# Two plain tile pairs behind the first six tiles of each FFN, with their weights, sums and output weights issued earlier

## The chip, the cores and the metric

The kernel runs on one core of one Trainium2 chip. The metric is device time in microseconds (us), the median of several runs; the kernel before takes 1227.42 us (three runs, 1227.06 to 1229.53). A profile is one further execution with its own time.

## The reference

One encoder layer runs over two independent sequences of 256 tokens, 1024 features, in float32:

```python
def encoder_layer(x, ...):
    x = x + 0.5 * swiglu(rmsnorm(x, g_ffn1), w_ffn1_in, w_ffn1_out)
    h = rmsnorm(x, g_mix)
    (q, k, v, r, lr, ml_qk, ml_v, ml_o, ml_if, gate_a, gate_b) = split(h @ w_in)
    o_a = gla_mixer(...)      # chunked linear attention, both directions, 4 heads
    o_b = mlstm_mixer(...)    # chunked mLSTM, both directions, 4 heads
    x = x + (sigmoid(gate_a) * o_a + sigmoid(gate_b) * o_b) @ w_out
    return x + 0.5 * swiglu(rmsnorm(x, g_ffn2), w_ffn2_in, w_ffn2_out)

def swiglu(h, w_in, w_out):   # w_in 1024 x 5632, w_out 2816 x 1024
    a, g = split(h @ w_in, 2)
    return (silu(a) * g) @ w_out
```

The result is `rmsnorm(x, g_final)` for each sequence. The change concerns the two FFNs (swiglu) and the passage from the mixers to the second.

## The kernel before

Activations are held transposed, features on 128 partitions and the 512 tokens of both sequences in the columns, as eight tiles `x[k]`. TensorE works on float32 in a rounded form (fp32r). To keep precision each operand is split into a high part (ScalarE's rounding copy, `split2` L223) and a low part (VectorE's difference, L224), and each product takes three matmuls: high by high, high by low, low by high (`mm3`, L201 to L204).

An FFN (`ffn`, L312) has 22 pairs of tiles: pair j is tile 2j of `a` and tile 2j + 1 of `g`, each 128 of the 2816 inner features.

*First tiles.* Pairs 0 to 2 are computed plainly (`first_tiles`, L226): six PSUM banks, eight k slices, and for each k 18 matmuls of 512 columns on `split_x(k)`, the input times its gain but not yet normalized. The weights come in four raw tiles of two slices (`kp`), and their split goes to a `wa` pair. Meanwhile the squares of x are summed (ScalarE squares, GpSimd adds, L199), and `rms_stat` (L176) turns them into `r`, the reciprocal root of each token's mean square: a matmul with ones (L160), a few small operations, four diagonals and another matmul (L173), and a copy. It is issued at high priority.

*Units.* Pairs 3 to 21 are each one step of a Winograd form of Strassen's product, called a unit here (L341 to L366). It takes seven products of 256 columns in place of eight: 7 x 4 x 3 = 84 matmuls (`product`, L296). It needs sums of the normalized inputs, `x_sums` (L248), four steps of VectorE and ScalarE work that need `r`, and sums of the pair's weights, `w_sums` (L276): three loads, VectorE sums (L286 to L289), splits, and, for the two blocks that are used unsummed, a low part made by ScalarE's negated copy (L284) and an accumulating DMA that adds the weights again from memory (L285, issued by GpSimd). The products go to banks `y`, `z` and `q`. Two products of a unit, `finish(late, 0)` and `finish(late, 1)`, run inside the next one.

*Output tiles.* After pairs 0 to 7, 8 to 14 and 15 to 21 the eight tiles of the output product are accumulated over that part's activations `hs` and added to x (L371 to L385).

What orders the work: the kernel is written in one sequence, and a planner places each engine's instructions by that sequence (earlier is more urgent), by its own estimate of times and by the buffers that are free. Each engine then runs its list in order and waits where an input is late. Buffers that the steps below touch: `slab`, 44 tiles of 512 columns (split inputs, sums, split activations); `tmp`, 7 tiles; PSUM with four banks `acc` and four `sc` (`acc(..., True)`); and in an FFN two each of `raw`, `sum` (loads, 3 x 512 columns), `wa` (high and low, 5 x 512) and `wb` (2 x 512).

Loads are issued on SP's queue, accumulating DMAs on GpSimd's. The mixers use other pools (`wp`, three each of raw, high, low weights) in the memory that the FFN pools leave. After the last mixer step comes the product with `w_out` (L816 to L820), and then the pools are changed back and the second FFN's first weights loaded (L824 to L833):

```python
    for i in range(KD):
        ps = gemm(w_out[i], ms, f"wo{i}", i % 2 == 1)
        nc.vector.tensor_tensor(out=x[i], in0=ps, in1=x[i], op=ALU.add)
        xs2.append(split_x(i, C_G2, sq_of("b"), "b"))
    mixer_stage.close()
    last_stage = ExitStack()
    last_stage.enter_context(pools(**ffn_pools))
    raw2 = []
```

Of the kernel before, what the change touches and what calls it, by code (L numbers as in the profile page):

```python
# [9 lines left out]
F32 = mybir.dt.float32  # L10
# [26 lines left out]
def encoder_kernel(ctx: ExitStack, tc: tile.TileContext, xT, par, w2, gnorm, mask,  # L37
# [117 lines left out]
    def rms_cols(parts, cs, name):  # L155

        ps = scp(f"st_{name}", (P, len(cs)))
# [8 lines left out]
    def spread(r, name):  # L166
# [5 lines left out]
        ps = scp(f"sp_{name}", (P, n * P))  # L172
# [53 lines left out]
    def first_tiles(raws, xs_of, name):  # L226
# [3 lines left out]
        for kp in range(4):  # L230
            raw = raws[kp].rearrange("p i m f -> p i (m f)")
            whi, wlo = (t.rearrange("p a b -> p (a b)")[:, :2 * NF * P].rearrange("p (i f) -> p i f", i=2)
                        for t in w_pair("wa", 5, f"{name}{kp}"))
            for i in range(2):
                k = 2 * kp + i
                split2(whi[:, i], wlo[:, i], raw[:, i])
# [3 lines left out]
                for m in range(NF):  # L240
                    nc.tensor.matmul(pss[m], lhsT=whi[:, i, f[m]], rhs=xh, start=k == 0, stop=False)
                for m in range(NF):
                    nc.tensor.matmul(pss[m], lhsT=wlo[:, i, f[m]], rhs=xh, start=False, stop=False)
                for m in range(NF):
                    nc.tensor.matmul(pss[m], lhsT=whi[:, i, f[m]], rhs=xl, start=False, stop=k == KD - 1)
        return pss

    def x_sums(gcol, r, name):  # L248

        res = [[] for _ in range(7)]  # L250
        b11 = None
        for k in range(4):
            u, v, t, w = (tmp(f"x{c}_{name}{k}") for c in "uvtw")
# [18 lines left out]
        return res  # L272
# [39 lines left out]
    def ffn(w_a, w_o, xs_of, raws, gcol, sq, name, done, last=None):  # L312

        pss = first_tiles(raws, xs_of, f"{name}i")
        r, _ = rms_stat(sq, name)
        sums = {n: w_sums(w_a, n, f"{name}s{n}") for n in (NF // 2,)}
        xc = x_sums(gcol, r, name)
        hs = []
        for j in range(NF // 2):
            t, g = tmp(f"{name}t{j}"), tmp(f"{name}g{j}")  # L320
            nc.vector.tensor_tensor(out=t, in0=pss[2 * j], in1=r, op=ALU.mult)  # L321
            nc.scalar.activation(t, t, AF.Silu)
            nc.vector.tensor_tensor(out=g, in0=pss[2 * j + 1], in1=r, op=ALU.mult)
            hs.append(activate(t, g, f"{name}{j}"))
        L, R = slice(0, SEQ), slice(SEQ, T)
        add = lambda o, p, q: nc.vector.tensor_tensor(out=o, in0=p, in1=q, op=ALU.add)
        late = None
# [10 lines left out]

        parts = [range(0, 8), range(8, 15), range(15, KF)]
        for part in parts:  # L340
            for j in part:  # L341
                if j < NF // 2:
                    continue
                w = sums.pop(j)
                if j + 1 < KF:
                    sums[j + 1] = w_sums(w_a, j + 1, f"{name}s{j + 1}")
                y, z = acc(f"psy_{name}{j}"), acc(f"psz_{name}{j}")
                m, u = tmp(f"{name}m{j}"), tmp(f"{name}u{j}")
                t, g = tmp(f"{name}t{j}"), tmp(f"{name}g{j}")
                product(y, w[0], xc[X11], True, False)  # L350
                nc.scalar.copy(m[:, L], y[:, :SEQ])  # L351
                product(z, w[1], xc[X21], True, True)
                add(t[:, L], z[:, :SEQ], m[:, L])
                nc.scalar.activation(t[:, L], t[:, L], AF.Silu)
                if late:
                    finish(late, 0)
                product(y, w[4], xc[XT2], False, False)
                nc.scalar.copy(u[:, R], y[:, :SEQ])
                if late:
                    finish(late, 1)  # L360
# [600 lines left out]
```

## Time and profile before

| | us |
|---|---|
| median of three runs | 1227.42 |
| the profiled execution | 1228.9 |
| its span, first to last instruction | 1227.1 |
| TensorE busy (matmuls) | 1183.4 |
| VectorE busy | 763.8 |
| ScalarE busy | 609.6 |
| GpSimd busy | 105.6 |

Busy time of TensorE counts each matmul from its start to its modelled end, and matmuls overlap, so a busy TensorE is not yet at its best rate; starts of neighbouring matmuls show the rate. In order of time the span holds: loads to 8 us, the first FFN to 377, the mixers to 805, the product with `w_out` to 850, the second FFN to 1206, and the final norm. In the rows, PE is TensorE's matmul, PEld its weight load, DVE VectorE, ACT ScalarE, POOL GpSimd, SP the queue that issues loads; L302 is line 302 of the kernel. Names carry f1 or f2 for the FFN, with `xh_a` or `xh_b` for the split inputs, `xch` and `xcl` for input sums, `wah`/`wal` and `wbh`/`wbl` for the high and low parts in `wa` and `wb`, and `ps_f1i`, `ps_f1o` for the banks of the first and of the output tiles.

### The profile page before, as it was taken

To read this page: it belongs to the slowest core of one execution; us is meant where nothing else is said; L and a number is where in the kernel's file an instruction comes from. 1 tells how busy PE (TensorE), PEld (TensorE's weight loads), DVE (VectorE), ACT (ScalarE), POOL (GpSimd) and SP (SyncE) were. 2 spreads that over 40 slices of the span, in tenths; PEclk is the share of its full clock that TensorE was granted. 3 is DMA by queue.
4 is the path that set the end of the run, shared out by engine and by line. 5 is a ranking of instruction groups with operands and counts; after the bars stand their busy time and mean duration, and the time that the engine had idled before them with its cause. 6 is when DMAs were issued, how large, how long until landed. Compare 5 with 4: busy or idle time off the path is not lost.

```text
span 1227.1 us, 17179 instructions
## 1 busy us (share of the span) xinstructions
PE 1183.4 (96%) x6795; PEld 1031.8 (84%) x6795; DVE 763.8 (62%) x1159; ACT 609.6 (50%) x997; POOL 105.6 (9%) x118
## 2 busy tenths in 40 slices
PE   7899999999999999999999999999989999999996
PEld 6788899889987887888888888887889899889985
DVE  6976367547645879657564463464987357656643
ACT  5655156426535655565762332343565156426541
POOL 4000000000012002111000000012000001000011
PEclk9889999999999999999999999998999999999998
DMA  7346356445523313232223333314355346535512
GB/s 235 78 115 161 103 123 166 124 120 130 149 84 107 89 50 99 80 114 61 95 77 103 95 95 112 95 60 132 86 128 155 101 116 161 141 101 145 154 45 69
DMA packets 56801, 136.65 MB, mean 111 GB/s; under 512 B 5192, under 2 KB 19528, under 8 KB 56720
## 3 DMA queue, kind: packets, MB, share of 16 engines
q1 hardware_dynamic: 48480, 110.38, 28.7%
q0 software_dynamic: 6432, 22.81, 10.9%
q10 hardware_dynamic: 1808, 2.36, 0.6%
q8 instruction: 53, 0.87, 0.3%
q14 instruction: 28, 0.23, 0.1%
HBM read 133.42 MB, written 2.11 MB: 110 GB/s over the span
## 4 chain that ended last, share of the span: by engine, by line
PE 86%; DVE 8%; ACT 2%; DMA 2%; issue 1%; POOL 0%; POOLq 0%; DVEq 0%; SPq 0%; ACTq 0%
PE psy_f L302 17%; PE psq_f L302 8%; PE psz_f L302 4%; PE ps_f1o L202 3%; PE ps_f1o L203 3%; PE ps_f1o L204 3%; PE ps_f2o L203 3%; PE ps_f2o L202 3%; PE ps_f2o L204 3%; PE pt_ga L465 2%; PE pt_ga L464 2%; PE pt_ga L466 2%; PE pt_gb L465 2%; PE pt_gb L464 2%; PE pt_gb L466 2%
## 5 line engine op out<-in xcount | busy, mean ns | idle before, releaser
L302 PE MATMUL psy_f<-xch_f,wah_f1s 128*128 128x256 f32 x228 | 65.2, 286 | 3.8 <-DVE f1t L321 1.4
L302 PE MATMUL psy_f<-xch_f,wal_f2s 128*128 128x256 f32 x228 | 64.9, 285 | 4.2 <-DMA wal_f2s<-in_w_f 4.2
L302 PE MATMUL psy_f<-xch_f,wah_f2s 128*128 128x256 f32 x228 | 64.5, 283 | 0.1
L302 PE MATMUL psy_f<-xcl_f,wah_f2s 128*128 128x256 f32 x228 | 64.5, 283 | 0.0
L302 PE MATMUL psy_f<-xch_f,wal_f1s 128*128 128x256 f32 x228 | 64.5, 284 | 0.0
L302 PE MATMUL psy_f<-xcl_f,wah_f1s 128*128 128x256 f32 x228 | 64.3, 282 | 0.0
L464 PE MATMUL pt_ga<-whi_ga,xh_m 128*128 128x512 f32 x128 | 50.7, 396 | 0.0
L465 PE MATMUL pt_ga<-wlo_ga,xh_m 128*128 128x512 f32 x128 | 50.7, 396 | 0.0
L465 PE MATMUL pt_gb<-wlo_gb,xh_m 128*128 128x512 f32 x128 | 50.6, 396 | 0.0
L464 PE MATMUL pt_gb<-whi_gb,xh_m 128*128 128x512 f32 x128 | 50.5, 394 | 0.0
L466 PE MATMUL pt_ga<-whi_ga,xl_m 128*128 128x512 f32 x128 | 50.4, 393 | 0.0
L466 PE MATMUL pt_gb<-whi_gb,xl_m 128*128 128x512 f32 x128 | 50.2, 393 | 0.0
L94 DVE TENSOR_TENSOR wlo_ga<-raw_ga,whi_ga 128x1024 fp32r<-128x1024 f32 x16 | 19.6, 1225 | 46.3 <-ACT whi_ga L93 46.3
L302 PEld LDWEIGHTS psy_f<-xch_f,wah_f1s 128*128 128x128 f32 x228 | 43.7, 192 | 5.0 <-DVE f1t L321 1.7
L302 PEld LDWEIGHTS psy_f<-xch_f,wal_f2s 128*128 128x128 f32 x228 | 43.4, 190 | 4.6 <-DMA wal_f2s<-in_w_f 4.6
L385 DVE SCALAR_TENSOR_TENSOR x<-ps_f2o,x 128x512 f32<-128x512 f32 x23 | 15.9, 690 | 49.2 <-PE ps_f2o L204 49.2
L385 DVE SCALAR_TENSOR_TENSOR x<-ps_f1o,x 128x512 f32<-128x512 f32 x24 | 16.6, 690 | 44.3 <-PE ps_f1o L204 44.3
L302 PEld LDWEIGHTS psy_f<-xcl_f,wah_f1s 128*128 128x128 f32 x228 | 43.8, 192 | 0.1
L302 PEld LDWEIGHTS psy_f<-xch_f,wah_f2s 128*128 128x128 f32 x228 | 43.3, 190 | 0.6 <-ACT f2m L351 0.5
L302 PEld LDWEIGHTS psy_f<-xch_f,wal_f1s 128*128 128x128 f32 x228 | 43.6, 191 | 0.0
L302 PEld LDWEIGHTS psy_f<-xcl_f,wah_f2s 128*128 128x128 f32 x228 | 43.3, 190 | 0.1
L94 DVE TENSOR_TENSOR wlo_gb<-raw_gb,whi_gb 128x1024 fp32r<-128x1024 f32 x16 | 19.6, 1223 | 36.1 <-ACT whi_gb L93 36.0
(1085 smaller groups left out, 4043.2 us busy)
## 6 DMA issues: line engine op xcount, KB each, us to landing
raw_f1s<-in_w_f SPq DMA_DIRECT2D x19, 512.0 KB, 3.7
wal_f1s<-in_w_f POOLq DMA_DIRECT2D x19, 512.0 KB, 5.6
raw_f2s<-in_w_f SPq DMA_DIRECT2D x19, 512.0 KB, 3.7
wal_f2s<-in_w_f POOLq DMA_DIRECT2D x19, 512.0 KB, 5.7
raw_ga<-in_w_tm SPq DMA_DIRECT2D x16, 512.0 KB, 3.6
raw_gb<-in_w_tm SPq DMA_DIRECT2D x16, 512.0 KB, 3.6
sum_f1s<-in_w_f SPq DMA_DIRECT2D x19, 256.0 KB, 3.2
raw_f1s<-in_w_f SPq DMA_DIRECT2D x19, 256.0 KB, 4.0
```

The source lines that it names most:

```text
L94: nc.vector.tensor_tensor(out=lo[:, :width], in0=raw[:, :width], in1=hi.bitcast(F32)[:, :width], op=ALU.subtract)
L202: nc.tensor.matmul(ps, lhsT=wh, rhs=xh, start=start, stop=False)
L203: nc.tensor.matmul(ps, lhsT=wh, rhs=xl, start=False, stop=False)
L204: nc.tensor.matmul(ps, lhsT=wl, rhs=xh, start=False, stop=stop)
L302: nc.tensor.matmul(ps, lhsT=l[:, f], rhs=m, start=start and k == n == 0, stop=stop and k == 3 and n == 2, skip_group_check=True)
L385: nc.vector.scalar_tensor_tensor(out=x[i], in0=ps, scalar=0.5, in1=x[i], op0=ALU.mult, op1=ALU.add)
L464: nc.tensor.matmul(pss[t], lhsT=xh, rhs=hi[:, ws], start=k == 0, stop=False)
L465: nc.tensor.matmul(pss[t], lhsT=xh, rhs=lo[:, ws], start=False, stop=False)
L466: nc.tensor.matmul(pss[t], lhsT=xl, rhs=hi[:, ws], start=False, stop=k == KD - 1)
```

## The change

Pairs 3 and 4 (`NP` and `NP + 1`) leave the units and become plain pairs, computed behind the first six tiles from the same split inputs; 17 units remain. Their weights are split by `split_dma`: high part by ScalarE, low part by its negated copy and an accumulating DMA. The first tiles use it too, from `kp` = 3 in the first FFN and from `kp` = 1 in the second, with the raw tile in SBUF as the DMA's source. Slices k = 0 and 1 of the first tiles are split into `wb` pairs. In the last slice the order of the matmuls is by bank, last bank first. The steps of `x_sums` are issued ahead of most of the scalings by `r` (`gated`); the activations (`act`) come behind both plain pairs. The body of a unit, now `pair`, and those of the output tiles, `w_out_tile` (load and split) and `out_tile` (matmuls and sum), are as before. Units and output tiles form one list, and the weights of the next entry are issued ahead of the work of the current one. Before the second FFN the pools `raw`, `sum`, `wb` are opened ahead of the product with `w_out`, whose loop issues the loads of the first tiles at i = 2 to 5; `wa` is opened behind it.

```diff
-    def rms_stat(sq, name):
+    def rms_stat(sq, name, banks=(None, None)):
         with tc.high_priority():
-            rc = rms_cols([sq], range(4), name)
-            ps = spread(rc, name)
+            rc = rms_cols([sq], range(4), name, banks[0])
+            ps = spread(rc, name, banks[1])
...
+    def split_dma(hi, lo, src, again):
+        nc.scalar.copy(hi, src)
+        nc.scalar.activation(lo, src, AF.Copy, scale=-1.0)
+        nc.gpsimd.dma_start(lo, again, accum_op=ALU.add)
+
-    def first_tiles(raws, xs_of, name):
+    def first_tiles(raws, xs_of, dma_from, name):
...
-            whi, wlo = (t.rearrange("p a b -> p (a b)")[:, :2 * NF * P].rearrange("p (i f) -> p i f", i=2)
-                        for t in w_pair("wa", 5, f"{name}{kp}"))
+            if kp:
+                wide = w_pair("wa", 5, f"{name}{kp}")
             for i in range(2):
                 k = 2 * kp + i
-                split2(whi[:, i], wlo[:, i], raw[:, i])
+                whi, wlo = (t.rearrange("p a b -> p (a b)")[:, i * NF * P:(i + 1) * NF * P]
+                            for t in wide) if kp else (t.rearrange("p a b -> p (a b)")[:, :NF * P]
+                                                       for t in w_pair("wb", 2, f"{name}{k}"))
+                if kp < dma_from:
+                    split2(whi, wlo, raw[:, i])
+                else:
+                    split_dma(whi, wlo, raw[:, i], raw[:, i])
...
+                passes = [(whi, xh), (wlo, xh), (whi, xl)]
+                order = [(m, n) for n in range(3) for m in range(NF)]
+                if k == KD - 1:
+                    order = [(m, n) for m in reversed(range(NF)) for n in range(3)]
...
     def x_sums(gcol, r, name):
...
         for k in range(4):
+            yield res
...
+    def w_plain(w_a, j, name):
+        raws = (stage["raw"].tile([P, 3, T], F32, tag="raw", name=f"raw_{name}"),
+                stage["sum"].tile([P, 3, T], F32, tag="sum", name=f"sum_{name}"))
+        res = []
+        for n, raw in enumerate(raws):
+            raw = raw[:, 0:2].rearrange("p a b -> p (a b)")
+            nc.sync.dma_start(raw, w_a[2 * j + n])
+            hi, lo = (p.rearrange("p a b -> p (a b)")[:, :2 * T]
+                      for p in w_pair("wb" if n else "wa", 2 if n else 5, f"{name}{n}"))
+            split_dma(hi, lo, raw, w_a[2 * j + n])
+            res.append((hi, lo))
+        return res
...
+        def pair(j, w):
...
+        NP = NF // 2
         parts = [range(0, 8), range(8, 15), range(15, KF)]
+        units = []
         for part in parts:
             for j in part:
...
+                if j >= NP + 2:
+                    units.append((lambda j=j: w_sums(w_a, j, f"{name}s{j}"), lambda w, j=j: pair(j, w)))
             for i in range(KD):
...
+                units.append((lambda part=part, i=i: w_out_tile(w_o, part, i, f"{name}o{part[0]}_{i}"),
+                              lambda w, part=part, i=i: out_tile(part, i, w)))
+        pss, xs = first_tiles(raws, xs_of, dma_from, f"{name}i")
+        banks = [[acc(f"ps_{name}p{n}", True) for n in range(2)]]
+        r, _ = rms_stat(sq, name, banks[0])
+        act_of = {}
+
+        def gated(j, a, b):
+            t, g = tmp(f"{name}t{j}"), tmp(f"{name}g{j}")
+            nc.vector.tensor_tensor(out=t, in0=a, in1=r, op=ALU.mult)
+            nc.scalar.activation(t, t, AF.Silu)
+            nc.vector.tensor_tensor(out=g, in0=b, in1=r, op=ALU.mult)
+            act_of[j] = t, g
+
+        def act(j):
+            act_of[j] = activate(*act_of[j], f"{name}{j}")
+
+        def plain(pss, w):
+            for ps, (hi, lo) in zip(pss, w):
+                for k in range(KD):
...
+                    mm3(ps, hi[:, f], lo[:, f], *xs[k], k == 0, k == KD - 1)
+
+        top = NP - 1
+        steps = x_sums(gcol, r, name)
+        for _ in range(3):
+            next(steps)
+        w_p = w_plain(w_a, NP, f"{name}p")
+        next(steps)
+        gated(top, pss[2 * top], pss[2 * top + 1])
+        xc += next(steps)
+        plain(banks[0], w_p)
+        w_p = w_plain(w_a, NP + 1, f"{name}p2")
+        gated(0, pss[0], pss[1])
+        nxt = units[0][0]()
+        banks.append([acc(f"ps_{name}p{n}", True) for n in range(2, 4)])
+        plain(banks[1], w_p)
+        gated(1, pss[2], pss[3])
+        for j in range(NP):
+            act(j)
+        for j in (NP, NP + 1):
+            gated(j, *banks[j - NP])
+            act(j)
+        hs += [act_of[j] for j in range(NP + 2)]
+        for n, (_, run) in enumerate(units):
+            cur, nxt = nxt, units[n + 1][0]() if n + 1 < len(units) else None
+            run(cur)
...
-    ffn(w_f1, w_o1, lambda k: split_x(k, C_G1, sq1, "a"), raw1, C_G1, sq1, "f1", done1)
+    ffn(w_f1, w_o1, lambda k: split_x(k, C_G1, sq1, "a"), raw1, 3, C_G1, sq1, "f1", done1)
...
     mixer_stage.close()
     last_stage = ExitStack()
-    last_stage.enter_context(pools(**ffn_pools))
+    last_stage.enter_context(pools(raw=2, sum=2, wb=2))
+    out_stage = ExitStack()
+    out_stage.enter_context(pools(wp=3))
...
+    xs2 = []
+    for i in range(KD):
+        if 2 <= i < 6:
+            second_raw(i - 2)
+        ps = gemm(w_out[i], ms, f"wo{i}", i % 2 == 1)
+        nc.vector.tensor_tensor(out=x[i], in0=ps, in1=x[i], op=ALU.add)
+        xs2.append(split_x(i, C_G2, sq_of("b"), "b"))
+    out_stage.close()
+    last_stage.enter_context(pools(wa=2))
...
-    ffn(w_f2, w_o2, lambda k: xs2[k], raw2, C_G2, sq_of("b"), "f2", done2, last2)
+    ffn(w_f2, w_o2, lambda k: xs2[k], raw2, 1, C_G2, sq_of("b"), "f2", done2, last2)
```

## Rows read from the trace of the kernel before

**Rows 1.** The page: span, and TensorE's busy time.

```profile
span 1227.1 us, 17179 instructions
...
PE 1183.4 (96%) x6795; PEld 1031.8 (84%) x6795; DVE 763.8 (62%) x1159; ACT 609.6 (50%) x997; POOL 105.6 (9%) x118
```

**Rows 2.** Table by stretch, around the units; columns in its first line.

```profile
core 0: us, PE busy (x) PEld busy (x) DVE busy (x) ACT busy (x) POOL busy (x), PEclk, DMA share, GB/s
48.28:115.28 67.00, 57.53 (x423) 55.02 (x422) 52.36 (x76) 40.82 (x63) 4.23 (x5) 0.90 0.52 128
888.63:948.42 59.79, 53.53 (x423) 52.03 (x422) 45.98 (x62) 37.84 (x58) 4.24 (x5) 0.97 0.59 147
159.36:230.34 70.98, 70.07 (x592) 69.78 (x590) 48.92 (x63) 43.68 (x67) 5.11 (x6) 1.00 0.62 154
268.82:339.62 70.80, 70.80 (x596) 70.39 (x594) 45.81 (x61) 41.35 (x65) 4.26 (x5) 1.00 0.58 145
992.44:1063.66 71.22, 70.31 (x592) 70.02 (x591) 49.12 (x63) 43.66 (x67) 5.11 (x6) 1.00 0.62 154
...
```

**Rows 3.** The same table, start of the units and output tiles, first FFN.

```profile
48.20:75.00 26.80, 19.19 (x112) 17.54 (x111) 24.90 (x40) 17.25 (x26) 1.69 (x2) 0.76 0.25 57
...
115.50:159.50 44.00, 44.00 (x192) 35.64 (x191) 20.95 (x23) 11.41 (x12) 0.85 (x1) 1.00 0.33 94
```

**Rows 4.** TensorE's waits: line, waited for, us, times, longest.

```profile
PE psy_f L302 <- DMA wal_f2s<-in_w_f: 4.2, 2, 2.9
...
PE psq_f L302 <- ACT xch_f L223: 2.4, 1, 2.4
...
PE ps_f1o L202 <- ACT wah_f1o L223: 1.9, 2, 1.0
...
PE psy_f L302 <- DVE f1t L321: 1.4, 1, 1.4
```

**Rows 5.** Timeline of TensorE, start of the second FFN; start, us, instruction, idle before.

```profile
850.20 2.71 PE L241 MATMUL ps_f2i<-xh_b,wah_f2i 128*128 128x512 f32 x6 [2.78 <-ACT wah_f2i L223]
...
863.58 1.52 PE L241 MATMUL ps_f2i<-xh_b,wah_f2i 128*128 128x512 f32 x6
```

**Rows 6.** Timeline from 29 to 55 us, VectorE and ScalarE.

```profile
29.02 0.68 DVE L286 TENSOR_TENSOR sum_f1s<-sum_f1s,raw_f1s 128x512 f32<-128x512 f32 x1
...
29.74 1.22 DVE L287 TENSOR_TENSOR sum_f1s<-sum_f1s,raw_f1s 128x1024 f32<-128x1024 f32 x1
...
31.08 0.75 DVE L255 SCALAR_TENSOR_TENSOR xu_f<-x,pt,r_f 128x512 f32<-128x512 f32 x1
...
32.41 0.42 DVE L258 TENSOR_TENSOR xt_f<-xu_f 128x256 f32<-128x256 f32 x1
...
35.16 0.42 DVE L224 TENSOR_TENSOR xcl_f<-xu_f,xch_f 128x256 fp32r<-128x256 f32 x1
...
35.83 0.69 DVE L224 TENSOR_TENSOR xcl_f<-xv_f,xch_f 128x512 fp32r<-128x512 f32 x1
...
39.00 1.06 ACT L284 ACTIVATE wal_f1s<-raw_f1s 128x1024 fp32r<-128x1024 f32 x1
...
42.61 1.76 DVE L224 TENSOR_TENSOR wal_f1s<-sum_f1s,wah_f1s 128x1536 fp32r<-128x1536 f32 x1
...
44.28 1.22 DVE L224 TENSOR_TENSOR wbl_f1s<-raw_f1s,wbh_f1s 128x1024 fp32r<-128x1024 f32 x1
...
54.38 0.68 DVE L321 TENSOR_TENSOR f1t<-ps_f1i,r_f 128x512 f32<-128x512 f32 x1
```

**Rows 7.** Line L285, all issues: duration in ns; landing in us.

```profile
L285 POOL DMA_DIRECT2D wal_f1s<-in_w_f x19: 842/847/888, 40.4 to 318.2; - x19
...
DMA to landing us min/median/max: 5.3/5.7/8.2
```

**Rows 8.** Timeline of TensorE, the first statistics product.

```profile
24.56 1.05 PE L160 MATMUL st_f<-ones,sq 128*128 128x1 f32 x8 [1.77 <-POOL sq L199]
```

**Rows 9.** Chain of waits, start and us.

```profile
70.17 2.93 PE psy_f L302 x12
```

More of the change, by code (lines that the diff above doesn't have):

```diff
@@ L153, in rsqrt, with rms_cols @@
         nc.vector.scalar_tensor_tensor(out=dst, in0=s, scalar=1.5, in1=dst, op0=ALU.add, op1=ALU.mult)
[L155 to L157 removed]
+    def rms_cols(parts, cs, name, bank=None):
+        ps = scp(f"st_{name}", (P, len(cs))) if bank is None else bank[:, :len(cs)]
         for i, c in enumerate(cs):
@@ L164, in rms_cols, with spread @@
         return r
-    def spread(r, name):
+    def spread(r, name, bank=None):
         n = r.shape[-1]
@@ L239, in first_tiles @@
                 f = [slice(m * P, (m + 1) * P) for m in range(NF)]
[L240 to L246, printed above, removed]
+                passes = [(whi, xh), (wlo, xh), (whi, xl)]
+                order = [(m, n) for n in range(3) for m in range(NF)]
+                if k == KD - 1:
+                    order = [(m, n) for m in reversed(range(NF)) for n in range(3)]
+                for m, n in order:
+                    w, xp = passes[n]
+                    nc.tensor.matmul(pss[m], lhsT=w[:, f[m]], rhs=xp, start=k == n == 0,
+                                     stop=k == KD - 1 and n == 2)
+        return pss, xs
     def x_sums(gcol, r, name):
@@ L310, in activate, with w_out_tile, ffn @@
         return h
[L312 to L324, printed above, removed]
+    def w_plain(w_a, j, name):
[10 more added lines that the diff above has]
+        return res
+    def w_out_tile(w_o, part, i, name):
+        n = len(part)
+        raw = (w_raw, w_sum)[i % 2](name).rearrange("p a b -> p (a b)")[:, :n * P]
+        nc.sync.dma_start(raw, w_o[i][:, part[0] * P:(part[-1] + 1) * P])
+        hi, lo = (c.rearrange("p a b -> p (a b)")[:, :n * P]
+                  for c in (w_pair("wa", 5, name) if i % 2 == 0 else w_pair("wb", 2, name)))
+        split2(hi, lo, raw)
+        return hi, lo
+    def ffn(w_a, w_o, xs_of, raws, dma_from, gcol, sq, name, done, last=None):
         L, R = slice(0, SEQ), slice(SEQ, T)
         add = lambda o, p, q: nc.vector.tensor_tensor(out=o, in0=p, in1=q, op=ALU.add)
-        late = None
+        late = []
+        hs = []
+        xc = []
         def finish(late, when):
@@ new lines, in out_tile @@
+        def out_tile(part, i, w):
+            if late:
+                finish(late[0], 0)
+                finish(late.pop(), 1)
+            hi, lo = w
+            n = len(part)
+            if last and part is parts[-1] and i == KD - 1:
+                last(hi, lo, hs)
+                return
+            ps = acc(f"ps_{name}o{part[0]}_{i}", i % 2 == 0)
+            for k in range(n):
+                f = slice(k * P, (k + 1) * P)
+                mm3(ps, hi[:, f], lo[:, f], *hs[k], k == 0, k == n - 1)
+            nc.vector.scalar_tensor_tensor(out=x[i], in0=ps, scalar=0.5, in1=x[i], op0=ALU.mult, op1=ALU.add)
+            if part is parts[-1]:
+                done(i)
+            if i == KD - 1:
+                hs.clear()
@@ L350, in ffn @@
[L350 to L360, printed above, removed]
```

65 lines of the change are left out of this document (23 added, 42 removed).

## The prediction

> **What bounds the kernel now.** The page's busy table comes first: TensorE is busy 1183.4 of 1227.1 us and VectorE, next, 763.8 [rows 1]. So the span is TensorE's work plus its stops, and a stage is worth what TensorE loses in it against the rate that it holds elsewhere. The second view is the table by stretch, cut at the Winograd units. The stretch 268.82 to 339.62 holds seven units: 596 matmuls in 70.80 us at a granted clock of 1.00, of which 588 are of 256 columns and 8 are early 512-column ones of the output tiles [rows 2]. A 512-column matmul takes 44.00/192 = 0.229 us [rows 3], so a unit takes (70.80 - 8 x 0.229)/7 = 9.85 us. I hold the other stretches against that:
> - 48.28 to 115.28, five units and 3 early matmuls: 5 x 9.85 + 0.7 = 49.95 us due, 67.00 taken: 17.05 lost, granted clock 0.90 [rows 2].
> - 888.63 to 948.42, the same in the second FFN: 59.79 taken, 9.84 lost, clock 0.97.
> - 159.36 to 230.34 and 992.44 to 1063.66, seven units and 4 early matmuls: 69.87 due, 70.98 and 71.22 taken: 1.11 and 1.35 lost.
> - 268.82 to 339.62: none, by definition.
> The third view, TensorE's waits, names the causes: 4.2 us on the low parts that an accumulating DMA brings, 2.4 us on ScalarE's high part of an input sum, 1.4 us on VectorE's scaling L321 (it frees the bank that psy needs), 1.9 us in two waits for the first output tile's high part [rows 4]. VectorE is busy 24.90 of 26.80 us from 48.20 to 75.00, and TensorE's clock there is 0.76 [rows 3]: the waits themselves are smaller than the loss, the rest is matmuls at the lower level (1.2 of 2.4 GHz) between waits. So the start of each FFN is set by VectorE, which must make the input sums before the first unit, while TensorE has only the first six tiles to run.
> Outside these stretches one more place matters: between the w_out product and the second FFN, TensorE idles 2.78 us on ScalarE's wah_f2i, and then takes 2.71 us for six matmuls where six later ones take 1.52 (each row with the same tail of its last matmul) [rows 5].
>
> **The change part by part.** The profiled execution took 1228.9 us, its span 1227.1; the sum is made on 1228.9. The median of the runs is 1227.4, 1.5 lower, and the 1.5 come off at the end.
> **A. Two plain pairs for two units, per FFN.** A plain pair is 2 tiles x 8 k x 3 passes = 48 matmuls of 512 columns: 48 x 0.229 = 11.0 us against 9.85. Four pairs: 4 x 1.15 = +4.6 us of TensorE time, on the path by its nature.
> **B. What stands behind the six tiles, FFN 1.** The pairs give TensorE 22.0 us that need only the split inputs xs, so VectorE's work for the first unit moves beside them. That work, from its first step on r at 31.1 us on: four input-sum steps, each 2 x 0.75 (L255) + 4 x 0.42 (L258) + one low part of 256 columns at 0.42 and three at 0.69 = 5.7 us, 22.7 in all; the first unit's weight sums, 0.68 + 1.22 + 0.69 + 1.76 + 1.22 = 5.6; four scalings of a pair at 2 x 0.68 = 5.4; sum 33.7 us [rows 6] (L289, the weight sums' third 512-column operation, taken at L286's duration). TensorE is busy until 48.3 + 22.0 = 70.3, so VectorE has 39.3 us for 33.7. The four causes of [rows 4] are then covered. What is late next is what can't start before the pairs end: all 44 slabs are held (16 by xs, 28 by the sums), so the activations' split outputs wait for xs to be released. Five activations (product and low part, 2 x 0.68 each: 6.8), one scaling (1.4) and the second unit's weight sums (5.6), with the unit's own three adds (1.3), fall into the 9.85 us of the first unit: 15.1, or 5.2 over. Part of it can slip into VectorE's spare 5.6 us or into the next two units. I take 3.0 us left over, between 0 and 6. Result 17.05 - 3.0 = -14.0 us.
> **C. The same in FFN 2:** 9.84 - 3.0 = -6.8 us. Here r comes earlier against the end of the tiles, but the bunch behind the pairs is the same.
> **D. Weights of the pairs by split_dma.** They cost VectorE nothing; ScalarE makes two passes of 1.06 us per tile, and the POOL queue's accumulating DMA is issued in 0.85 and lands in 5.7 (5.3 to 8.2) [rows 6, 7]. The first tile's wa buffer comes free when the tiles' k = 5 is done, 36 matmuls or 8.3 us before the pair is due: 1.06 + 1.06 + 5.7 = 7.8, so 0.5 of margin at the median and 2.0 us late at the slowest landing. That lies inside the 3.0 of B and C. The DMA waits in POOL's queue behind the square sums and for ScalarE; behind it stand the later low parts only.
> The Trainium skill's page "SBUF — State Buffer", section "Who interferes with whom", speaks against this: a DMA issued from GpSimd needs its descriptors written through a port pair that VectorE can hold. In the stretch where VectorE is 93% busy, POOL's two issues still take 1.69/2 = 0.85 us [rows 3, 7], so the row shows no hold. By the rule, read at its hardest, each issue could wait out a 1.76 us operation, the first plain tile would be 1.3 us late in each FFN, and the forecast would be 1208 rather than 1206.
> **E. Start of FFN 2.** The raw tiles are loaded during the w_out product into memory that the mixer's weight pool has left, and the first two k slices are split into wb buffers that don't overlap the ones in use. So the 2.78 us wait goes, and with it the slow matmuls behind it: from 850.20 to 863.58 are 13.4 us for 36 matmuls, 8.2 at 0.229, and two statistics products, about 1.9 by the first one's 1.05 [rows 5, 8], so 3.3 lost. Full gain 6.1 us. It is less if the low part of k = 2 is late, whose buffer is free only with the end of the w_out product: two ScalarE passes of 1.06 x 768/1024 = 0.8 and a landing of 5.7 (or 8.2) make 7.3 (9.8) us, and the 36 matmuls of k = 0 and 1 and the six of k = 2's high part cover 9.6. I take -4.5, between 0 and -6.1. The eight loads that move into SP's queue between the w_out loads I take at nothing; one w_out load that lands late behind them would cost up to a landing less the product's lead, 3 us, which the range holds.
> **F. Weights a unit ahead.** The waits for the first output tile (about 1.0 and 0.9 per FFN): the first of each is inside B and C; of the second, 1.11 + 1.35, I take half, -1.2 (0 to -2.5). For FFN 1's kp = 3 and FFN 2's kp = 1 to 3 the low parts leave VectorE; that gives it time that B and C already count as spare.
> **G. First tiles of FFN 1.** The stop for the square sums, 1.77 us [rows 8], is ahead of the new work. kp = 0 in wb lets ScalarE reach the squares earlier; kp = 3 now waits for a wa buffer. I take nothing, between -1.8 and +1.
> Sum: +4.6 - 14.0 - 6.8 - 4.5 - 1.2 = -21.9 us: 1207.0 by the profiled execution, 1205.5 by the median; forecast **1206 us**.
>
> **The rivals.**
> 1. *Everything is covered.* No remainder in B and C, full E and F: 4.6 - 17.05 - 9.84 - 6.1 - 2.5 = -30.9: 1196.5. For it: VectorE's 5.6 us of spare. Against: the 15.1 us bunch. With G too it would be 1195.
> 2. *VectorE stays the bound, half is recovered.* The weights or the sums come late in the order in which ScalarE serves them, and each wait brings the lower clock back, as from 48 to 75 us now: 4.6 - 8.5 - 4.9 - 4.5 = -13.3: 1214. For it: the margins of D; against: 39 us for 34 of work.
> 3. *The order doesn't do what it says.* The planner that writes the engines' orders places the pairs where TensorE waits anyway later, the losses of B and C stay, only E is gained: +4.6 - 4.5 = 0.1: 1227.5.
> 4. *Slower: the buffers close the chain.* Six of seven temporaries are held by the three scaled pairs until their activations run, these wait for slabs, which wait for the end of the second plain pair; the third pair's scaling needs a temporary and frees the bank that the first unit's psq needs. If VectorE's queue holds all of this and the weight sums in front of what the unit needs, TensorE waits 6.8 + 2.7 + 5.6 = 15.1 us, and then runs a unit at the lower clock: twelve matmuls took 2.93 us at 70.17 [rows 9] where twelve of a unit's 84 are due 1.41, which for some 28 matmuls is 3.5 us. 18.6 per FFN gives 4.6 - 17.05 - 9.84 - 1.2 - 4.5 + 37.2 = +9.2: 1237. It decides from 14.0 us per FFN on, where the sum is nought. For it: slabs and temporaries are exactly used up. Against: psq stands third in the unit, some 4 us in, and needs one activation and one scaling, 2.7 us, not all.
>
> **How the numbers follow.** Forecast 0.50 (with its own range 1200 to 1210), rival 1 0.15, rival 2 0.18, rival 3 0.07, rival 4 0.10. The range takes in the first three: 1195 to 1221; rivals 3 and 4, 0.17, are left out. A change of 0.2%, 2.5 us, is what a measurement of this kernel tells from none. Faster is the forecast and rivals 1 and 2: 0.83; rival 3 is split between same and slower: same 0.06, slower 0.11.
>
> **What would show it.** The two stretches behind the first tiles should hold 96 plain matmuls at 0.229 us and then three units at 9.85 with at most some 3 us lost, at a granted clock of 1.00; a clock under 0.95 there speaks for rivals 2 or 4. VectorE's input sums should end before the second pair does. The wait for wah_f2i should be gone and the six first matmuls of the second FFN take about 1.5 us. The two waits for the first output tile should go. The forecast is wrong if TensorE waits on DMA wal of the pairs or on activations for over 6 us per FFN.

## The result and the profile after

The changed kernel takes 1208.13 us (median of 4 runs, 1207.70 to 1209.11), the kernel before beside it 1228.27 (4 runs): a ratio of 0.9838, 95% interval 0.9825 to 0.9851. The forecast was 1206, with a range of 1195 to 1221. The profiled execution took 1207.96 us, its span is 1206.2; the terms below are made on spans, 1227.1 - 1206.2 = 20.9 us.

The page of the changed kernel: the span, and TensorE's busy time [rows 1]. TensorE has 144 matmuls fewer and is busy 6.0 us less; the other 14.9 us were time in which it stood idle.

```profile
span 1206.2 us, 16870 instructions
...
PE 1177.4 (98%) x6651; PEld 1019.8 (85%) x6651; DVE 736.0 (61%) x1127; ACT 609.0 (50%) x989; POOL 114.9 (10%) x130
```

The table by stretch of the changed kernel: plain pairs and the three units of the first FFN, the same of the second, then the seven units of each second part [rows 2].

```profile
core 0: us, PE busy (x) PEld busy (x) DVE busy (x) ACT busy (x) POOL busy (x), PEclk, DMA share, GB/s
47.01:71.32 24.31, 22.55 (x98) 17.95 (x96) 21.79 (x34) 16.28 (x23) 2.54 (x3) 1.00 0.69 163
71.32:102.65 31.33, 31.33 (x259) 30.83 (x258) 18.29 (x25) 16.03 (x27) 0.85 (x1) 1.00 0.54 135
867.81:897.65 29.84, 24.91 (x98) 19.73 (x96) 24.02 (x36) 17.06 (x23) 2.55 (x3) 0.89 0.44 103
897.65:928.97 31.32, 31.32 (x259) 30.81 (x258) 18.06 (x25) 16.23 (x27) 0.86 (x1) 1.00 0.52 137
145.75:216.57 70.82, 70.82 (x595) 70.42 (x594) 45.73 (x60) 41.37 (x65) 4.26 (x5) 1.00 0.58 144
972.12:1042.97 70.85, 70.85 (x595) 70.45 (x594) 45.68 (x60) 41.40 (x65) 4.26 (x5) 1.00 0.57 144
```

Two pairs without a wait take 22.3 us (22.27 to 22.30 in experiments below). So the first FFN's pairs lose some 2.0 us, the second's 7.5, the latter partly at the lower clock (mean granted clock 0.89). For the units, a count such as x259 has to be read with care: it takes in matmuls that only lap over an edge of the stretch. Of the 596 in [rows 2] six are early ones of the output tiles and two only lap over, so at 22.27/96 = 0.232 us for a 512-column matmul a unit takes (70.80 - 6 x 0.232)/7 = 9.92 us; in the timelines units follow each other 9.91 to 9.92 us apart. Here there are six early ones in each stretch: three units are due 3 x 9.92 + 6 x 0.232 = 31.15 us and take 31.33 and 31.32, so they lose 0.2 us; seven are due 70.83 and lose nothing any more.

TensorE's waits in the changed kernel: of those of [rows 4] none is left, and two new ones stand there, both on the low part of the second pair's first tile. (The third line, on the diagonals of the statistics, is not new: the kernel before waits 1.43 us there.)

```profile
PE ps_f2p L204 <- DMA wal_f2p<-in_w_f: 4.9, 1, 4.9
...
PE ps_f1p L204 <- DMA wal_f1p<-in_w_f: 1.8, 1, 1.8
PE ps_f1p L173 <- DVE dg_f L171: 1.5, 1, 1.5
```

TensorE's timeline, first FFN's statistics [rows 8] and the start of the second FFN [rows 5]: the first statistics matmul waits for nothing now, the second still for the diagonals; the first six tiles run right behind the w_out product and take 1.56 us, the same tail included.

```profile
23.25 1.05 PE L160 MATMUL ps_f1p<-ones,sq 128*128 128x1 f32 x8
...
27.94 1.10 PE L173 MATMUL ps_f1p<-dg_f,ones 128*128 128x512 f32 x2 [1.46 <-DVE dg_f L171]
...
832.32 0.40 PE L204 MATMUL ps_wo<-mh,wlo_wo 128*128 128x512 f32 x1
832.55 1.56 PE L258 MATMUL ps_f2i<-xh_b,wbh_f2i 128*128 128x512 f32 x6
```

Where the 4.9 us come from is read backwards, queue by queue, in the second FFN. TensorE waits for the low part; GpSimd issued it only at 876.85; ScalarE's negated copy for it ran at 875.50, behind a Silu (its table load is the row L431) for which ScalarE had idled 10.55 us; that Silu waited for VectorE's scaling L430; and VectorE had idled 10.90 us, because the planner had put the first unit's weight sum L302 ahead of that scaling, and its loads were not there. VectorE, ScalarE, GpSimd and TensorE in the timeline:

```profile
869.99 0.69 DVE L302 TENSOR_TENSOR sum_f2s<-sum_f2s,raw_f2s 128x512 f32<-128x512 f32 x1 [10.90 <-DMA raw_f2s<-in_w_f]
870.60 0.68 DVE L430 TENSOR_TENSOR f2t<-ps_f2i,r_f 128x512 f32<-128x512 f32 x1
...
871.38 1.28 ACT L431 ACT_TABLE_LOAD   x1 [10.55 <-DVE f2t L430]
...
874.03 1.05 ACT L228 CAST wah_f2p<-raw_f2p 128x1024 fp32r<-128x1024 f32 x1
...
875.50 1.05 ACT L229 ACTIVATE wal_f2p<-raw_f2p 128x1024 fp32r<-128x1024 f32 x1
...
876.85 0.85 POOL L230 DMA_DIRECT2D wal_f2p<-in_w_f  x1 [16.31 <-ACT wal_f2p L229]
...
884.51 0.80 PE L204 MATMUL ps_f2p<-xh_b,wal_f2p 128*128 128x512 f32 x1 [4.93 <-DMA wal_f2p<-in_w_f]
```

The loads were late as well, and for a reason that the change brought: the accumulating DMAs of the first tiles read the raw weights where they lie, so that buffer is held until they have landed. SP's waits, 845 to 880 us:

```profile
SPq L296 <- DMA wal_f2i<-sum_second: 11.5, 1, 11.5
```

And SP's timeline: the first of the four loads goes out at 860.57; in the trace the last of those DMAs lands at 860.45.

```profile
860.57 0.83 SPq L296 DMA_DIRECT2D sum_f2s<-in_w_f  x2
```

This hold is the smaller part: in x6 below, where VectorE makes those low parts, VectorE still idles 9.2 us at this place.

In the first FFN this idle time isn't there; the second pair's low part is issued at 51.36 us and lands 9.1 us later, the slowest of the four landings (first tiles of both pairs, line L230; the first FFN, then the second):

```profile
DMA to landing us min/median/max: 5.5/7.3/9.1
...
DMA to landing us min/median/max: 7.3/7.5/7.6
```

### The profile page after: what moved, and what is told of

Read it like the earlier page. It is cut to its first block, busy times and chain, and to the rows that moved or that the text cites. A ratio compares the mean times of both kernels' runs of the same rounds, so it can differ in the third digit from the quotient of the medians.

```text
span 1206.2 us, 16870 instructions
## 1 busy us (share of the span) xinstructions
PE 1177.4 (98%) x6651; PEld 1019.8 (85%) x6651; DVE 736.0 (61%) x1127; ACT 609.0 (50%) x989; POOL 114.9 (10%) x130
## 4 chain that ended last, share of the span: by engine, by line
PE 89%; DVE 5%; DMA 2%; issue 2%; ACT 1%; SPq 1%; POOL 0%; POOLq 0%; DVEq 0%
PE psy_f L318 16%; PE psq_f L318 8%; PE psz_f L318 4%; PE ps_f1o L203 3%; PE ps_f1o L204 3%; PE ps_f1o L202 3%; PE ps_f2o L203 3%; PE ps_f2o L202 3%; PE ps_f2o L204 3%; PE ps_f2i L258 3%; PE pt_ga L545 2%; PE pt_ga L543 2%; PE pt_ga L544 2%; PE pt_gb L545 2%; PE pt_gb L543 2%; PE pt_gb L544 2%
## 5 line engine op out<-in xcount | busy, mean ns | idle before, releaser
L318 PE MATMUL psy_f<-xch_f,wal_f1s 128*128 128x256 f32 x204 | 57.3, 281 | 0.0
L318 PE MATMUL psy_f<-xcl_f,wah_f1s 128*128 128x256 f32 x204 | 57.2, 281 | 0.0
L318 PE MATMUL psy_f<-xch_f,wah_f2s 128*128 128x256 f32 x204 | 57.2, 281 | 0.0
L318 PE MATMUL psy_f<-xcl_f,wah_f2s 128*128 128x256 f32 x204 | 57.2, 281 | 0.0
L318 PE MATMUL psy_f<-xch_f,wal_f2s 128*128 128x256 f32 x204 | 57.2, 280 | 0.0
L318 PE MATMUL psy_f<-xch_f,wah_f1s 128*128 128x256 f32 x204 | 57.2, 281 | 0.0
L93 ACT CAST whi_gb<-raw_gb 128x1024 fp32r<-128x1024 f32 x16 | 16.8, 1048 | 45.7 <-PE pt_ga L545 29.5
L318 PEld LDWEIGHTS psy_f<-xch_f,wah_f1s 128*128 128x128 f32 x204 | 38.4, 189 | 0.1
L318 PEld LDWEIGHTS psy_f<-xcl_f,wah_f1s 128*128 128x128 f32 x204 | 38.4, 188 | 0.1
L318 PEld LDWEIGHTS psy_f<-xch_f,wal_f1s 128*128 128x128 f32 x204 | 38.5, 189 | 0.0
```

Of the source, the lines that this page charges most:

```text
L93: nc.scalar.copy(hi[:, :width], raw[:, :width])
L318: nc.tensor.matmul(ps, lhsT=l[:, f], rhs=m, start=start and k == n == 0, stop=stop and k == 3 and n == 2, skip_group_check=True)
```

## The experiments

Each differs from the changed kernel only by the edit shown or named, has four or five runs, and is compared with the changed kernel's 1208.13 us. They were run in three batches (x1, x2, x3, x5; x4, x6, x7, x8; x9 to x12), with medians of the kernel before of 1228.0, 1228.9 and 1229.0 beside 1228.27 for the changed kernel's; so a difference of 1 or 2 us between batches rests on the traces rather than on the medians.

| experiment | us (range) | ratio to before, 95% |
|---|---|---|
| x1 weight sums behind the scaling | 1200.63 (1199.02 to 1200.70) | 0.9774 (0.9760 to 0.9789) |
| x2 second pair's low part by VectorE | 1203.10 (1201.60 to 1204.98) | 0.9798 (0.9781 to 0.9815) |
| x3 no plain pairs | 1215.98 (1213.70 to 1217.22) | 0.9900 (0.9885 to 0.9915) |
| x5 old passage from w_out | 1216.33 (1214.47 to 1217.05) | 0.9903 (0.9888 to 0.9918) |
| x4 weights not ahead | 1208.68 (1208.01 to 1209.25) | 0.9838 (0.9822 to 0.9853) |
| x6 first tiles by VectorE | 1205.91 (1204.13 to 1206.90) | 0.9817 (0.9801 to 0.9832) |
| x7 x1 and x2 | 1199.38 (1198.89 to 1199.67) | 0.9762 (0.9747 to 0.9777) |
| x8 x1, low parts from SBUF | 1205.06 (1204.00 to 1206.16) | 0.9809 (0.9793 to 0.9824) |
| x9 x1, x2 in the first FFN alone | 1198.96 (1198.42 to 1199.35) | 0.9755 (0.9733 to 0.9777) |
| x10 x1, x6 in the first FFN alone | 1199.13 (1198.19 to 1199.70) | 0.9756 (0.9733 to 0.9778) |
| x11 x1, one pair per FFN | 1212.63 (1210.38 to 1213.77) | 0.9864 (0.9840 to 0.9888) |
| x12 no weights ahead, old order at a boundary | 1208.16 (1207.18 to 1210.21) | 0.9831 (0.9807 to 0.9854) |

**x1: is it the order of VectorE's list?** The first unit's weight sums are held behind the scaling of the top pair of the first tiles.

```diff
-        gated(top, pss[2 * top], pss[2 * top + 1])
+        scaled = gated(top, pss[2 * top], pss[2 * top + 1])
...
-        nxt = units[0][0]()
+        with tc.issue_after(scaled):
+            nxt = units[0][0]()
```

> The changed kernel, with the first unit's weight sums on VectorE held behind the scaling of the last of the first six tiles' pairs (nothing else moved). Theory 1 (order): in FFN 2 the sum L302 stands on VectorE ahead of that scaling and waits 10.9 us for a load; through the scaling it holds ScalarE's Silu and the copies of the second plain pair, whose low part then lands 4.9 us late. Expected: the wait on wal_f2p under 1 us, about 1201.5 us (1208.1 less 5 to 7.4), FFN 1 as it was. Theory 2 (the DMA itself): it lands in 7.3 to 9.1 us in either FFN because the first unit's loads run beside it, whatever VectorE's order: at least 3 us of the wait stay, 1205.5 us or more.

The order it was. VectorE scales as soon as the bank is done, the sums follow; the second FFN's pairs take 22.30 us at a granted clock of 1.00, and 29.84 - 22.30 = 7.5 us is the whole gain. The first FFN keeps its loss. VectorE's timeline of this kernel, and then its table by stretch:

```profile
865.15 0.69 DVE L430 TENSOR_TENSOR f2t<-ps_f2i,r_f 128x512 f32<-128x512 f32 x1 [6.21 <-PE ps_f2i L258]
...
872.35 0.69 DVE L302 TENSOR_TENSOR sum_f2s<-sum_f2s,raw_f2s 128x512 f32<-128x512 f32 x1
```

```profile
46.77:71.02 24.25, 22.55 (x97) 17.96 (x96) 21.80 (x34) 16.29 (x23) 2.54 (x3) 1.00 0.72 164
867.73:890.03 22.30, 22.30 (x98) 18.06 (x96) 21.55 (x33) 15.50 (x22) 2.56 (x3) 1.00 0.56 141
```

**x2: the disputed low part by VectorE.** `split2` in place of `split_dma` for the first tile of the second pair.

> The changed kernel, with the low part of the second plain pair's first tile made by VectorE's difference in place of the accumulating DMA, order of the sums left. Theories 1 and 2 both: the waits on that low part go in both FFNs (1.8 and 4.9 us, with the slow matmuls behind them 1.9 and 7.4): about 1199.5 us. Theory 3 (VectorE's bunch, the one of the prediction): the 1.2 us more on VectorE and the work behind the pairs make the first units wait in its place, half of the gain is lost: 1204 us.

Both waits go (22.27 and 22.29 us), yet the kernel lies between the two expectations. VectorE's idle time, which this edit leaves in, comes out elsewhere: in the second FFN's units TensorE waits on a copy of ScalarE, whose list has fallen behind. The stretch of the three units takes 37.35 us at a granted clock of 0.91, 6.0 us more than in the changed kernel. (The profiled execution took 1204.33 us; the four runs lie at 1201.6, 1201.9, 1204.3 and 1205.0.) Timeline of TensorE, and the table by stretch:

```profile
893.93 0.58 PE L318 MATMUL psy_f<-xch_f,wah_f2s 128*128 128x256 f32 x1 [2.89 <-ACT f2m L377]
```

```profile
888.04:925.39 37.35, 34.46 (x260) 33.56 (x258) 23.39 (x32) 19.84 (x32) 1.71 (x2) 0.91 0.48 119
```

**x3: no plain pairs**, pairs 3 and 4 as units again (and the statistics back in banks of their own).

```diff
-                if j >= NP + 2:
+                if j >= NP:
...
-        plain(banks[0], w_p)
...
-        plain(banks[1], w_p)
```

> The changed kernel without any plain pair: pairs 3 and 4 are units again, all else as in the change. If the pairs are what covers VectorE's work, the losses behind the first tiles return (16.0 and 8.8 us without the boundary waits, in place of 1.9 and 7.4) and the price of the pairs (4.6) goes: 1219 us. If issuing the input sums ahead of the scalings is what helps, about half of that returns: 1211 us or less.

The pairs are worth 7.9 us as they stand, 3 less than expected. Without them the 396 unit matmuls up to the first output tile, due 46.8 us at 9.92 a unit, lose 13.3 and 9.4 us; the same stretches of the kernel before, 63.59 and 56.39 us long, lose 16.8 and 9.6. So in the first FFN 3.5 us of the gain stay without any pair; which other part of the change brings them was not tried. The old kind of wait is back in both FFNs (table by stretch, TensorE's waits):

```profile
47.69:107.78 60.09, 51.41 (x397) 50.18 (x396) 46.63 (x65) 34.71 (x55) 3.39 (x4) 0.94 0.53 132
877.45:933.63 56.18, 51.16 (x397) 50.29 (x396) 41.56 (x60) 34.40 (x55) 3.42 (x4) 0.94 0.54 134
```

```profile
PE psy_f L318 <- DVE f1t L429: 3.6, 1, 3.6
...
PE psy_f L318 <- DVE f2t L429: 2.1, 1, 2.1
```

**x5: the pools and loads of the second FFN's first tiles behind the w_out product again.**

> The changed kernel with the pools and loads of FFN 2's first tiles behind the w_out product again. If that early part gives what the traces show at its place (w_out product 45.28 to 42.21 us, first tiles 38.43 to 35.26), 6.2 us come back: 1214.3 us. Rival: a later start of FFN 2 only takes up time in which the second pair's low part is late anyway (4.9 us): 1210 us.

8.2 us slower: the 2.8 us wait is back in front of the first tiles, with matmuls at the lower clock behind it, 6.1 us in all. The other 2 us lie in the first FFN's pairs, which the edit doesn't touch: 26.24 us there, with a wait of 2.1 us and a granted clock of 0.93, where the changed kernel has 1.8 us at 1.00. So a wait of that size may or may not bring the lower clock, and the first FFN's loss in the pairs is 1.9 to 3.9 us from kernel to kernel.

**x4: no weights ahead.**

```diff
-            cur, nxt = nxt, units[n + 1][0]() if n + 1 < len(units) else None
-            run(cur)
+            run(nxt if n == 0 else units[n][0]())
```

> The weights of each later unit are made when its turn comes, not a unit ahead; all else as changed. Theory: the waits at the boundaries for the first output tile come back, 1.1 and 1.35 us at the second boundary of each FFN and about 1 us at the first: 1208.1 + 2.4 to 4 = 1210.5 to 1212 us. Rival: with the pairs in front the engines that make the weights have room, and the weights ahead give nothing: 1208 us.

No change, and no wait at a boundary. In this kernel the first output tile's weights still stood in front of the last products of the unit before it; **x12** puts them behind, as in the kernel before.

```diff
...
+            if late and n and (n + 1 == len(units) or tile_of[n]):
+                finish(late[0], 0)
+                finish(late.pop(), 1)
+            run(nxt if n == 0 else units[n][0]())
```

> No weights ahead, and the first output tile's weights are issued behind the last products of the unit before it, as in the kernel before (without the weights ahead alone they still stood in front of these). Theory: that order made the waits at the boundaries: they come back with some 1 us at each of the four, 1208.7 + 2.4 to 4 = 1211 to 1213 us. Rival: the boundary waits went because VectorE and ScalarE are no longer behind after the pairs: 1208.7 us.

Again no change, so neither of the two made the gain at the boundaries. What still differs from the kernel before is the order in which the weights are made. There a unit's weights were already made a unit ahead, but those of the next part's first unit came before the output tiles': its first high part takes a `wa` buffer at 216.05 us. In front of the first output tile's, at 225.95, ScalarE sits idle for 0.81 us until a product on psy is done: the one other `wa` buffer is in use by the unit that runs. So it is the buffer that comes late, and TensorE waits for that. Timelines of ScalarE and TensorE, the kernel before:

```profile
216.05 1.05 ACT L283 CAST wah_f1s<-raw_f1s 128x1024 fp32r<-128x1024 f32 x1 [0.49 <-PE psy_f L302]
...
225.95 0.94 ACT L223 CAST wah_f1o<-raw_f1o 128x896 fp32r<-128x896 f32 x1 [0.81 <-PE psy_f L302]
...
226.94 0.50 PE L202 MATMUL ps_f1o<-f18hh,wah_f1o 128*128 128x512 f32 x1 [0.91 <-ACT wah_f1o L223]
```

In x12, as in the changed kernel, the weights are made in the order of use: the first output tile's take the buffer that comes free a unit earlier, and their high part is there 9 us before it is needed:

```profile
202.95 0.95 ACT L223 CAST wah_f1o<-raw_f1o 128x896 fp32r<-128x896 f32 x1 [0.83 <-PE psy_f L318]
...
212.78 0.39 PE L202 MATMUL ps_f1o<-f18hh,wah_f1o 128*128 128x512 f32 x1
```

That the order of use is the cause fits these rows; it was not tried by itself.

**x6: the first tiles' low parts by VectorE**, four k slices in either FFN.

```diff
-    ffn(..., raw1, 3, C_G1, ...)
+    ffn(..., raw1, 4, C_G1, ...)
...
-    ffn(..., raw2, 1, C_G2, ...)
+    ffn(..., raw2, 4, C_G2, ...)
```

> The low parts of the first tiles that accumulating transfers bring (the last of the first FFN's four k slices, three of the second FFN's) are made by VectorE again; the plain pairs' and the units' stay on transfers. Theory: VectorE idles 10.9 us ahead of the second FFN's plain pairs, so nothing changes there: 1207 to 1209 us. Rival 1: fewer transfers on the queue let those of the plain pairs land sooner, and the 1.8 and 4.9 us of waits shrink: 1205 us or less. Rival 2: VectorE is late with the low parts in the first tiles (some 1.5 us for each slice): 1210 us or more.

2.2 us faster by the medians, little more than their scatter, and just short of the 1205 us of the first rival; the profiled execution (1204.13) is the fastest of the five. The trace shows the gain where that rival said: the first FFN's wait is gone (22.30 us; the DMA is issued at 50.32 and lands 7.8 us later). In the second the wait shrinks from 4.9 to 3.9 us and VectorE's idle time from 10.9 to 9.2: the raw buffer is free sooner, but the order fault stays.

**x8: x1, with the pairs' accumulating DMAs reading the raw weights in SBUF.**

```diff
-            split_dma(hi, lo, raw, w_a[2 * j + n])
+            split_dma(hi, lo, raw, raw)
```

> The order of the first experiment (weight sums behind the scaling), and the plain pairs' accumulating transfers read the raw weights from SBUF, where they already are, rather than from HBM again. Theory 1: a landing's 5.5 to 9.1 us is set by the transfer engines that other loads share; the source makes no difference, the first FFN's wait of 1.7 us stays: 1200.6 us. Theory 2: the read from HBM makes the landing long; it falls below 5 us, the wait goes: 1198.7 us.

Theory 2 was right that the landing gets shorter (if not below 5 us in the second FFN) and wrong on the time. The landings of the two tiles fall from 5.5 and 9.1 us to these, in the first FFN and then the second:

```profile
DMA to landing us min/median/max: 4.6/4.8/5.0
...
DMA to landing us min/median/max: 5.0/5.4/5.7
```

(In x1 the second FFN's were 7.2 and 7.5.) But the kernel is 4.4 us slower than x1. The planner places the first pair's copy later (the DMA is issued at 44.53 in place of 40.10 us), the *first* plain tile now waits in both FFNs, 1.8 and 2.0 us, and the pairs take 25.93 and 24.53 us:

```profile
46.72:72.65 25.93, 24.12 (x97) 19.10 (x96) 24.67 (x39) 17.71 (x24) 2.55 (x3) 0.93 0.78 191
869.71:894.24 24.53, 22.56 (x97) 17.98 (x96) 20.93 (x32) 15.46 (x21) 2.56 (x3) 1.00 0.70 177
```

The later issue muddies the comparison of the landings, too. One of the four stands in the same place in both kernels, 3.7 us into the second FFN's pairs, and there the landing is 7.5 us in x1 and 5.7 here. A shorter transfer is no gain when the list gives it a later place. That a source in SBUF with the old place gains was not tried.

**x7, x9, x10: what is left in the first FFN.**

> Both edits at once: the first unit's weight sums behind the scaling of the first plain pair, and the low part of the second pair's first tile by VectorE. Theory: the two waits are separate. Alone, the order took away the second FFN's wait (plain stretch 22.30 us) and left 1.7 to 1.9 us in the first FFN, where the transfer itself lands late; VectorE's low part takes these away. So 1200.6 - 1.9 = 1198.7 us. Rival: VectorE has no room for the two low parts (about 0.6 us each), and what they delay comes back as a wait on ScalarE's activation copy in the second FFN's units, as when VectorE made the low parts alone (2.9 us there): 1200.6 or more, with a loss of 2 us or more in the units.

> The first unit's weight sums behind the scaling of the first plain pair in both FFNs, and VectorE's low part for the second pair's first tile in the first FFN alone. With VectorE's low part in both, the first FFN's plain stretch took 22.27 us and the second's 23.32 (a wait of 0.76 us). Theory: what VectorE has to spare differs from FFN to FFN, so each gets the kind that loses nothing: both stretches at 22.3 us, 1199.4 - 1.2 = 1198.2 us. Rival: the remainder in the second FFN doesn't come from VectorE: 1199.4.

> The weight sums behind the scaling, and in the first FFN the last of the four k slices of the first tiles gets its low parts from VectorE instead of two accumulating transfers. With this in both FFNs the second pair's low part in the first FFN was issued 1.0 us sooner and landed 7.8 instead of 9.1 us after its issue, and the wait of 1.8 us was gone. Theory: that was the queue and the transfers in it, and it adds to the order's gain: 1200.6 - 1.9 = 1198.7 us. Rival: it needed the old order of the sums: 1200.6 us.

x7: the first FFN's pairs 22.27 us, the second's 23.32, with a wait of 0.8 us there, on the first pair's low part, which landed 9.5 us after its issue. x9 and x10, which leave the second FFN as in x1, have both at 22.3 to 22.6 us and a clock of 1.00. All three come nearer to the theories' 1198.2 to 1198.7 us than to x1's 1200.6; x9 can't be told from its rival of 1199.4. The medians of x9 and x10, 1198.96 and 1199.13, lie under four of x1's five runs, but the intervals of the ratios overlap with x1's: that the first FFN's wait is gone is shown by the traces, that this is worth 1.5 us only made likely by the times. Between x7, x9 and x10 the ranges overlap. They are the fastest kernels found, 9 us under the changed one. The table by stretch of x9:

```profile
46.91:69.18 22.27, 22.27 (x97) 18.04 (x96) 21.62 (x34) 15.39 (x22) 1.69 (x2) 1.00 0.67 157
866.13:888.74 22.61, 22.56 (x97) 17.98 (x96) 21.23 (x33) 15.51 (x22) 2.56 (x3) 1.00 0.59 139
```

**x11: one plain pair per FFN**, with x1's order.

> One plain pair for one unit in each FFN instead of two, with the sums behind the scaling. Theory: the pairs are cover for VectorE's 33.7 us. With one, TensorE is busy until 47.0 + 11.15 = 58.2 us in the first FFN and VectorE until 31.1 + 33.7 = 64.8: 6.6 us lost there and some 3 of slow matmuls behind it, less 1.3 for the dearer pair and 1.9 for the transfer that is no longer waited for; in the second FFN, where 9.5 us were lost without pairs, one pair of 11.15 covers all: 1200.6 + 9.6 - 1.9 - 2.6 = 1205.7 us, between 1202 and 1208. Rival: the second pair covers nothing that the first doesn't: 1200.6 - 1.9 - 2.6 = 1196.1 us.

Far outside: 12 us slower than x1. In the first FFN the 312 unit matmuls up to the first output tile, in 43.70 us, lose 6.9 where 6.6 and some 3 were expected for the units: VectorE does need the second pair as cover there. In the second FFN, where one pair should have been enough, the same stretch takes 46.20 us and loses 9.4, and this tells nothing of cover: VectorE idled again for a weight sum ahead of the scaling. The edit holds only the first unit's sums behind it. The first unit's loads had landed by 859.7 us; this sum waits for the next set of loads, issued from 866.25 and landed at 874.15, so it is the second unit's, which the edit doesn't hold. VectorE's timeline of x11:

```profile
874.27 0.69 DVE L302 TENSOR_TENSOR sum_f2s<-sum_f2s,raw_f2s 128x512 f32<-128x512 f32 x1 [10.30 <-DMA raw_f2s<-in_w_f]
874.88 0.68 DVE L430 TENSOR_TENSOR f2t<-ps_f2i,r_f 128x512 f32<-128x512 f32 x1
```

## Why the prediction was right, and which terms were not

The direction, the mechanism (plain pairs as cover for VectorE) and the sum held. That the sum came within some 2 us of the measured time is luck in part: C gave 4.8 us less than predicted, and B, E, F and G together gave 4.5 us more.

| step | predicted | measured |
|---|---|---|
| A, price of the pairs | +4.6 | 4 x (11.15 - 9.92) = +4.9 |
| B, first FFN's loss | -14.0 (3.0 left) | 16.9 to 2.2 = -14.7 |
| C, second FFN's loss | -6.8 (3.0 left) | 9.7 to 7.7 = -2.0 |
| E, start of the second FFN | -4.5 | -6.2 |
| F, second boundaries, units and output tiles | -1.2 | 109.46 to 108.60, 109.64 to 108.59: -1.9 |
| G, first FFN's first tiles | 0 | -1.4 |

With +0.5 in the tail the measured terms make -20.8, against -20.9 of the spans and -21.9 predicted. The measured column uses 9.92 us for a unit and 0.232 for a 512-column matmul. The prediction's 9.85 and 0.229 are a little low, since its counts of matmuls take in those that only lap over an edge: it read 8 early ones where there are six, and 3 and 4 where there are two. That moves none of its terms by more than 0.3 us.

**C is the step that failed**, with B beside it in its reason. The 3.0 us left over were put down to VectorE's bunch behind the pairs, 15.1 us of work in the first unit. It isn't there: in the 9.85 us from the first unit's start, 71.32 to 81.17, VectorE is busy for 6.5 of 9.85 us, since most of the scalings and activations fit beside the pairs, and no unit waits. What was left over is one transfer, in D's territory: D priced the low part of the first pair's first tile (0.5 us of margin; by the landings at 45.84 and 867.03 it was 1.2 and 0.8) and none for the second pair's, whose copies stand in ScalarE's list behind the Silu of the scaled first tiles. The prediction followed the buffer of the first DMA and not the list in front of the second. x1 shows that in the second FFN the place of one VectorE instruction is worth 7.5 us; x9 and x10 show that the first FFN's 2 us are a landing of 9.1 us, and go when VectorE makes this low part (x9) or when two accumulating DMAs ahead of it are taken away, with an issue 0.5 us sooner and a landing of 7.7 us (x10). One of the prediction's own signs pointed the same way: a granted clock under 0.95 behind the first tiles was to speak for rivals 2 or 4, and the second FFN's pairs had 0.89.

**A, B and E** are confirmed by undoing: x3 costs 7.9 us, x5 6.1 in its place. Of B some 3.5 us are not the pairs' (x3). E came in full, also because the wait and the slow matmuls behind it go together, as it said. **G** was taken at nothing, though it named what came: with k = 0 and 1 in `wb` ScalarE makes the last square at 19.75 us and not at 21.17, and the statistics product starts at 23.25 and not at 24.56. That no stop is left in front of it is owed to slow matmuls at the start, a granted clock of 0.89 from 8.14 to 23.25; in x5 the clock is 1.00 there, the stop is 1.53 us, and the first tiles take as long (38.84 us against 38.87). The wait for the diagonals is as before, 1.46 after 1.43. **F** lay within its range, but not for its reason: x4 and x12 show that weights a unit ahead gain nothing here, and the kernel before had them ahead for its units.

**On D's rule** (the Trainium skill, page "SBUF — State Buffer", section "Who interferes with whom"), by which VectorE can hold up the descriptors of a DMA that GpSimd issues: D read it as if any operation of VectorE could. That section of the Trainium skill names copies, casts and tensor_scalar in a mode that uses both ports, and infers that tensor_tensor does not stop the writing of descriptors. In the first FFN's pairs 32 of VectorE's 34 operations are TENSOR_TENSOR, and the other two only lap over the start of the stretch. VectorE is busy 21.79 of 24.31 us there, and GpSimd's issues take 0.84 to 0.85 us in the timeline, as in the kernel before. So the trace agrees with that inference, under which D's 1208 us does not follow, and no run here shows whether other operations hold an issue. The landings behind the issues vary, 5.5 to 9.1 us; what makes them vary was not found.

**Of the rivals**, 1 (all covered, 1196.5) is what x9 and x10 come near, at 1199; the 15.1 us bunch that spoke against it was no obstacle there. 2 had the right kind of cause, weights late in the order in which ScalarE serves them, at one place rather than all over. 3 and 4 did not come: the pairs cover, and no buffer closes the chain.

## What to carry to other kernels

A stage with work to spare on every engine can still be set by one instruction at the head of an in-order list: when filler work is put in front of a bottleneck, follow each engine's list to the *last* thing that the filler needs, and ask of every item ahead of it what it waits for. A DMA that reads a buffer holds it until it lands, so a low part that costs no engine time can delay the next loads. And test a gain by undoing the part it is credited to: the weights ahead would have had the credit for a gain that stays without them.

## What the runs showed of the hardware

An accumulating DMA of 512 KB landed 5.5 to 9.1 us after its issue when it read its weights from memory again (x1), and 4.6 to 5.7 us when it read the same weights from SBUF (x8); three of the four were issued at other moments, the fourth, in the same place, went from 7.5 to 5.7. A source in SBUF alone does not make a landing short: the first tiles' DMAs of 384 KB, which read SBUF, took 3.9 to 8.2 us in the changed kernel.

The length of a stop of TensorE did not alone decide whether the lower clock followed. In the plain pairs a wait of 1.8 us left the granted clock at 1.00 in the first FFN of the changed kernel and came with 0.93 in x8, one of 2.0 us left it at 1.00 in the second FFN of x8, one of 2.1 came with 0.93 (x5) and one of 4.9 with 0.89.
